# Adding the squares of the new x on VectorE before TensorE takes their column sums

## The chip, the cores and the metric

The kernel runs on one NeuronCore of a Trainium2 chip. The metric is device time in microseconds, from the start to the end of one execution. The profile names the engines PE (TensorE's matmuls), PEld (TensorE's weight loads), DVE (VectorE), ACT (ScalarE), POOL (GpSimd) and SP (SyncE, which issues the DMAs).

## The reference

A two-layer decoder trunk on 512 tokens of 1024 features, in float32. Layer 0 mixes tokens with dilated attention and an S5 state-space layer side by side, layer 1 with a gated linear recurrence (RG-LRU). Each mixer is followed by a SwiGLU feed-forward with 2816 hidden features.

```python
def rms_norm(x, g):
    return x * rsqrt(mean(x * x, axis=-1, keepdims=True) + 1e-6) * g

for layer in range(2):
    hn = rms_norm(x, norm_mix_pre[layer])
    mix = even_mixer(hn, ...) if layer % 2 == 0 else odd_mixer(hn, ...)   # both end in  y @ w_out
    x = x + rms_norm(mix, norm_mix_post[layer])
    hn = rms_norm(x, norm_ffn_pre[layer])
    ff = (silu(hn @ w_gate[layer]) * (hn @ w_up[layer])) @ w_down[layer]
    x = x + rms_norm(ff, norm_ffn_post[layer])
```

So there are four places where a product is normed, added to x, and the new x is normed again for the next stage. Three of them go through the function that is changed here; the fourth, behind the last feed-forward, writes the output and has no next norm.

## The kernel before

x is kept transposed: eight tiles `xT[f]` of 128 features (partitions) by 512 tokens. A float32 product is made of three matmuls of split operands, high times high, low times high, high times low; so each weight and each activation has a `hi` part, which ScalarE writes, and a `lo` part, which VectorE writes as the difference.

`out_proj` (L414) makes the output projection of a stage, the norm after it, the addition to x and the operands of the next stage. It is called three times: for layer 0's mixer (its tiles read `mo`, the products that follow `mo0b`), for layer 0's feed-forward (`fd`, then `fd0b`) and for layer 1's mixer (`mo` again, then `mo1b`). Below, these are mo0, fd and mo1. The product of the last four weight rows is done for the two halves of the tokens one after the other, 256 columns each, and `norm_half(h)` (L472) then works on half h while TensorE goes on with the other half, and after that with the next stage's products of the half that is done (`half_cols`, L549).

For a half, `cs` (L170 through `col_sums`) sums the squares of the product o over the features; `rst` on VectorE (L378 or L380) and `rsy` on POOL (L381) make the reciprocal root of it; `bc` broadcasts it over the partitions by TensorE. Then, for each of eight feature tiles f:

- L490, VectorE: o = o * gain * bc
- L496, POOL (for f = 0 VectorE, L494): xT += o
- L497, ScalarE: `xh`, the high part of the next operand
- L500, ScalarE: the square of the new x, into `nsq`
- L485, VectorE: `xl`, the low part, some tiles later

The squares must be summed over all 1024 features for the norm ahead of the next stage. TensorE does it: `next_sums` (L468) takes, for each tile and each 128 tokens, the square as the weights and a column of ones as the moving operand, and adds up in the bank `ns`. That is 16 matmuls for a half, 32 for a call, 96 in all; each leaves two records in the trace. They are issued for two tiles together, one pair of tiles late, so that the squares are mostly ready. When a call's `ns` is complete, `rst_f` (or `rst_m`), `rsy_f` and `bc_f` follow from it as above.

TensorE, VectorE and ScalarE each take their instructions strictly in their own queue's order. While `in_order` is set, which is from the tail of the projection through the first `half_cols` of the next stage, the instructions of `out_proj` on these engines keep the order in which the program states them (`pe.pin`, `seq_of`). When the steps of `norm_half` come in between the matmuls is set by due times on a clock that counts the matmuls stated with `pe.matmul` (`NORM_CS`, `NORM_BC`, `NORM_F`); `next_sums` states its own with `pe.pin` and moves no clock. All other instructions, those of the feed-forward and of layer 1, are placed by a scheduler, and shift when its picture of the engines shifts.

The two feed-forwards follow mo0 and mo1. They make most of their products by the Winograd form of Strassen's scheme (seven products of half blocks), so VectorE forms sums of weights (L638 to L641) and of activations (L660 to L663), ScalarE casts them to high parts (`whi`, L240; `th`, L667) and VectorE makes the low parts (`wlo`, L241; `tl`, L668). Behind fd stand plain products for layer 1, of 512 columns each.

## Time and profile before

| | |
|---|---|
| time, median of 3 runs | 1176.76 us (1175.7 to 1180.08) |
| profiled execution | 1172.18 us |
| its span | 1170.2 us |
| mean granted TensorE clock | 0.995 |
| busy: PE, PEld, DVE, ACT, POOL | 1129.9, 1010.3, 878.1, 629.2, 60.5 us |
| first and last group of `ns` matmuls starts in mo0, fd, mo1 | 266.5 and 290.5, 626.4 and 651.8, 797.2 and 824.3 us |

The span runs from the first to the last instruction on the profile's clock; the execution's own time is 2.0 us longer. "Busy" of an engine is the time in which at least one of its instructions runs. An idle time in square brackets at a row's end names the instruction that ended it. Times of single rows are from the span's start.

### The profile page before, as it was taken

The numbers are of one execution on the slowest core, as the hardware profiler recorded it, in microseconds if no ns is written. First come the engines' busy times: TensorE is split into PE (matmuls) and PEld (weight loads), VectorE is DVE, ScalarE is ACT, GpSimd is POOL, SyncE is SP. The second block draws the span as 40 slices with busy tenths as digits, with TensorE's granted clock in tenths as the row PEclk, the third lists the DMA queues.
The fourth block names the chain that finished last, engine by engine and source line by source line (L and its number), as shares of the span: only waits on it lengthen the run. The fifth ranks groups of instructions, "written<-read, shape, count | busy, mean of one in ns | idle before, by whom it ended". The sixth has DMA issues, their size and how long they took to land.

```text
span 1170.2 us, 20253 instructions
## 1 busy us (share of the span) xinstructions
PE 1129.9 (97%) x7550; PEld 1010.3 (86%) x7550; DVE 878.1 (75%) x1841; ACT 629.2 (54%) x1290; POOL 60.5 (5%) x101
## 2 busy tenths in 40 slices
PE   6899999999999999999999999999999999999997
PEld 6777766789899999988889987889999999988886
DVE  7978875567999899983445896966999899994224
ACT  7556567446754545662243469744955455582221
POOL 2000010004000000000002200004000000000001
PEclk9899999999999999999999999999999999999999
DMA  8254420431343323332340333340253343234221
GB/s 214 97 147 123 104 73 1 141 95 28 110 119 97 91 85 106 94 121 92 114 121 1 91 91 90 121 132 1 73 144 95 91 118 95 85 123 123 93 63 72
DMA packets 165273, 113.45 MB, mean 97 GB/s; under 512 B 26820, under 2 KB 141752, under 8 KB 165176
## 3 DMA queue, kind: packets, MB, share of 16 engines
q1 hardware_dynamic: 161848, 109.94, 32.2%
q10 hardware_dynamic: 3040, 2.17, 0.7%
q8 instruction: 59, 0.97, 0.4%
q14 instruction: 38, 0.31, 0.1%
q0 software_dynamic: 288, 0.07, 0.0%
HBM read 103.75 MB, written 4.19 MB: 92 GB/s over the span
## 4 chain that ended last, share of the span: by engine, by line
PE 78%; ACT 8%; DMA 6%; DVE 5%; issue 2%; POOL 1%; SPq 0%; ACTq 0%; DVEq 0%; POOLq 0%
PE fo L170 10%; PE op_fd L170 10%; PE qkv L170 5%; PE f00b L170 5%; PE f02b L170 5%; PE f01b L170 4%; PE f11b L170 4%; PE op_mo L170 4%; PE f12b L170 4%; PE f10b L170 4%; PE gg L170 3%; PE f03b L170 2%; PE f13b L170 2%; PE xbb L170 2%; PE fd0b L170 2%
## 5 line engine op out<-in xcount | busy, mean ns | idle before, releaser
L241 DVE TENSOR_TENSOR wlo_fo<-wraw_fo,whi_fo 128x512 fp32r<-128x512 f32 x44 | 30.2, 691 | 63.6 <-PE fo L170 55.4
L170 PE MATMUL op_fd<-hi_f,whi_fd 128*128 128x512 f32 (+1 forms) x200 | 73.6, 368 | 0.0
L170 PE MATMUL op_fd<-lo_f,whi_fd 128*128 128x512 f32 (+1 forms) x200 | 73.3, 366 | 0.0
L170 PE MATMUL op_fd<-hi_f,wlo_fd 128*128 128x512 f32 (+1 forms) x200 | 72.9, 368 | 0.0
L170 PE MATMUL fo<-wlo_fo,hi_f 128*128 128x512 f32 x176 | 69.6, 395 | 0.0
L170 PE MATMUL fo<-whi_fo,lo_f 128*128 128x512 f32 x176 | 69.2, 394 | 0.0
L170 PE MATMUL fo<-whi_fo,hi_f 128*128 128x512 f32 x176 | 68.9, 396 | 0.0
L240 ACT ACTIVATE whi_fo<-wraw_fo 128x512 fp32r<-128x512 f32 x44 | 27.6, 631 | 70.2 <-DMA wraw_fo<-in_ffn_w_down_dram 43.8
L241 DVE TENSOR_TENSOR wlo_fd<-wraw_fd,whi_fd 128x512 fp32r<-128x512 f32 x44 | 30.0, 690 | 46.5 <-ACT whi_fd L240 40.4
L240 ACT ACTIVATE whi_fd<-wraw_fd 128x512 fp32r<-128x512 f32 x44 | 27.4, 629 | 55.0 <-DMA wraw_fd<-in_ffn_w_down_dram 34.2
L170 PEld LDWEIGHTS op_fd<-lo_f,whi_fd 128*128 128x128 f32 x200 | 37.7, 189 | 6.9
L170 PE MATMUL qkv<-whi_qkv,xh_m 128*128 128x512 f32 x96 | 42.1, 440 | 1.5 <-DVE up L1200 1.3
L170 PEld LDWEIGHTS op_fd<-hi_f,wlo_fd 128*128 128x128 f32 x200 | 37.7, 188 | 6.7
L170 PEld LDWEIGHTS op_fd<-hi_f,whi_fd 128*128 128x128 f32 x200 | 37.7, 188 | 6.5
L170 PE MATMUL qkv<-wlo_qkv,xh_m 128*128 128x512 f32 x96 | 39.2, 408 | 2.6 <-DVE wlo_qkv L241 2.6
L170 PEld LDWEIGHTS fo<-whi_fo,lo_f 128*128 128x128 f32 x176 | 33.1, 188 | 7.8
L170 PEld LDWEIGHTS fo<-whi_fo,hi_f 128*128 128x128 f32 x176 | 33.1, 188 | 7.7
L170 PEld LDWEIGHTS fo<-wlo_fo,hi_f 128*128 128x128 f32 x176 | 33.1, 188 | 7.5
L170 PE MATMUL qkv<-whi_qkv,xl_m 128*128 128x512 f32 x96 | 39.0, 407 | 0.0
L638 DVE TENSOR_TENSOR wraw_s_f<-wraw_f,wraw_f 128x512 f32<-128x512 f32 x40 | 27.3, 683 | 10.6 <-DMA wraw_f<-in_ffn_w_up_dram 7.5
L241 DVE TENSOR_TENSOR wlo_mo<-wraw_mo,whi_mo 128x512 fp32r<-128x512 f32 x32 | 21.4, 685 | 15.3 <-ACT whi_mo L240 15.1
L639 DVE TENSOR_TENSOR wraw_t_f<-wraw_s_f,wraw_f 128x512 f32<-128x512 f32 x40 | 27.2, 681 | 5.6 <-DMA wraw_f<-in_ffn_w_gate_dram 5.6
(1975 smaller groups left out, 4289.2 us busy)
## 6 DMA issues: line engine op xcount, KB each, us to landing
wraw_f<-in_ffn_w_gate_dram SPq DMA_DIRECT2D x88, 256.0 KB, 3.2
wraw_f<-in_ffn_w_up_dram SPq DMA_DIRECT2D x88, 256.0 KB, 3.4
wraw_fd<-in_ffn_w_down_dram SPq DMA_DIRECT2D x44, 256.0 KB, 2.7
wraw_fo<-in_ffn_w_down_dram SPq DMA_DIRECT2D x44, 256.0 KB, 2.9
wraw_qkv<-in_ev_w_in_dram SPq DMA_DIRECT2D x24, 256.0 KB, 3.5
wraw_mo<-in_ev_w_out_dram SPq DMA_DIRECT2D x16, 256.0 KB, 5.2
wraw_xb<-in_od_w_in_dram SPq DMA_DIRECT2D x16, 256.0 KB, 2.9
wraw_gg<-in_od_w_in_dram SPq DMA_DIRECT2D x16, 256.0 KB, 2.9
```

Of the source, the lines that this page charges most:

```text
L170: self.pin(nc.tensor.matmul(o, lhsT=lhsT, rhs=rhs, start=start, stop=stop, **kw))
L240: act.activation(hi, src, AF.Copy)
L241: eng.tensor_tensor(lo, src, hi.bitcast(F32), op=ALU.subtract)
L638: dve.tensor_tensor(s1, a21, a22, op=ALU.add)
L639: dve.tensor_tensor(s2, s1, a11, op=ALU.subtract)
```

## The change

The squares get four buffers for each half, of 128 by 256. Tile 0's square goes into the fourth, `sq[3]`, which then serves as the running total; the others rotate through the first three. VectorE adds each square to the total, one tile late (the add of tile f−1 is stated after the square of tile f), seven adds for a half. When the total is complete, TensorE takes its column sums with two matmuls, one for each 128 tokens, which start and stop by themselves. So a half has 2 `ns` matmuls and not 16, and 7 adds; over three calls 84 matmuls go and 42 adds come. Squares, xh, xl, o and POOL's adds are the same in number. Behind L500 line numbers become six smaller.

```diff
-        def next_sums(h, fs, q):
-            for i, f in enumerate(fs):
-                for t in range(2):
-                    c = 2 * h + t
-                    pe.pin(nc.tensor.matmul(nsum[:, c:c + 1], lhsT=q[:, i * HT + t * P:i * HT + (t + 1) * P],
-                                            rhs=ones[:, 0:1], start=(c == 0 and f == 0), stop=(f == NF - 1),
-                                            skip_group_check=True))
...
+            sq = [sb.tile([P, S], F32, tag="sqacc" if h else "sq", bufs=2, name=f"nsq_{nm}{h}{i}") for i in range(2)]
+            sq = [q[:, HS[i]] for q in sq for i in range(2)]
...
-                if f % 2 == 0:
-                    q = sb.tile([P, S], F32, tag="sqacc" if h else "sq", bufs=2, name=f"nsq_{nm}{h}{f}")
-                seq_of(act.activation(q[:, HS[f % 2]], xf, AF.Square))
+                seq_of(act.activation(sq[f % 3] if f else sq[3], xf, AF.Square))
+                if f > 1:
+                    seq_of(dve.tensor_tensor(sq[3], sq[3], sq[(f - 1) % 3], op=ALU.add))
                 late.append(f)
-                if f % 2 and f > 1:
-                    next_sums(h, (f - 3, f - 2), qlast)
-                if f % 2:
-                    qlast = q
                 ready.update((h, q) for q in range(late[0]))
                 yield NORM_F
-            next_sums(h, (NF - 2, NF - 1), qlast)
+            seq_of(dve.tensor_tensor(sq[3], sq[3], sq[(NF - 1) % 3], op=ALU.add))
+            for t in range(2):
+                c = 2 * h + t
+                pe.pin(nc.tensor.matmul(nsum[:, c:c + 1], lhsT=sq[3][:, t * P:(t + 1) * P], rhs=ones[:, 0:1],
+                                        start=True, stop=True))
```

VectorE's queue in fd, from o of tile 4 of the first half (`o_fd_7376` before, `o_fd_7358` after) to the o of tile 7; `rst` belongs to the second half. Before:

```order
L490 SCALAR_TENSOR_TENSOR o_fd_7376<-o_fd_7376,cols,bc_fd_7588 128x256
L485 SCALAR_TENSOR_TENSOR xl_fd_7442<-xT_179,cols,xh_fd_7434 128x256
L490 SCALAR_TENSOR_TENSOR o_fd_7378<-o_fd_7378,cols,bc_fd_7588 128x256
L485 SCALAR_TENSOR_TENSOR xl_fd_7443<-xT_180,cols,xh_fd_7435 128x256
L490 SCALAR_TENSOR_TENSOR o_fd_7380<-o_fd_7380,cols,bc_fd_7588 128x256
L485 SCALAR_TENSOR_TENSOR xl_fd_7444<-xT_181,cols,xh_fd_7436 128x256
L380 SCALAR_TENSOR_TENSOR rst_fd_7729<-cs_fd_7724,eps_f_3386 128x2
L490 SCALAR_TENSOR_TENSOR o_fd_7382<-o_fd_7382,cols,bc_fd_7588 128x256
```

and after:

```order
L484 SCALAR_TENSOR_TENSOR o_fd_7358<-o_fd_7358,cols,bc_fd_7570 128x256
L479 SCALAR_TENSOR_TENSOR xl_fd_7424<-xT_179,cols,xh_fd_7416 128x256
L494 TENSOR_TENSOR nsq_fd_7574<-nsq_fd_7574,nsq_fd_7573 128x256
L484 SCALAR_TENSOR_TENSOR o_fd_7360<-o_fd_7360,cols,bc_fd_7570 128x256
L479 SCALAR_TENSOR_TENSOR xl_fd_7425<-xT_180,cols,xh_fd_7417 128x256
L494 TENSOR_TENSOR nsq_fd_7574<-nsq_fd_7574,nsq_fd_7573 128x256
L484 SCALAR_TENSOR_TENSOR o_fd_7362<-o_fd_7362,cols,bc_fd_7570 128x256
L479 SCALAR_TENSOR_TENSOR xl_fd_7426<-xT_181,cols,xh_fd_7418 128x256
L494 TENSOR_TENSOR nsq_fd_7574<-nsq_fd_7574 128x256
L380 SCALAR_TENSOR_TENSOR rst_fd_7706<-cs_fd_7701,eps_f_3368 128x2
L484 SCALAR_TENSOR_TENSOR o_fd_7364<-o_fd_7364,cols,bc_fd_7570 128x256
```

Between every two o now stands an add of a square, the square of the tile ahead of the last o; `rst` stands behind the add of tile 5's square. The order of mo1 is the same.

TensorE's queue in fd at the sums of the first half (`fd0b` are products of layer 1 from tiles that are done), before:

```order
L170 MATMUL fd0b_7669<-xh_fd_7435,whi_xb_0_7412 128x256
L170 MATMUL fd0b_7669<-xh_fd_7435,wlo_xb_0_7413 128x256
L468 MATMUL ns_fd_7448<-ones,nsq_fd_7718 128x1 x4
L170 MATMUL fd0b_7670<-xh_fd_7435,whi_xb_0_7424 128x256
L170 MATMUL fd0b_7670<-xh_fd_7435,wlo_xb_0_7425 128x256
```

and after:

```order
L170 MATMUL fd0b_7649<-xh_fd_7417,whi_xb_0_7394 128x256
L170 MATMUL fd0b_7649<-xh_fd_7417,wlo_xb_0_7395 128x256
L501 MATMUL ns_fd_7430<-ones,nsq_fd_7574 128x1 x2
L170 MATMUL fd0b_7650<-xh_fd_7417,whi_xb_0_7406 128x256
L170 MATMUL fd0b_7650<-xh_fd_7417,wlo_xb_0_7407 128x256
```

The last sums of the half keep their place among the products of tile 3, ahead of the `bc` of the second half; three groups of four ahead of them are gone.

VectorE's queue at the end of mo0's second half, where the feed-forward's work begins (`wraw`, `wlo` are weights). Before:

```order
L490 SCALAR_TENSOR_TENSOR o_mo_2936<-o_mo_2936,cols,bc_mo_3272 128x256
L485 SCALAR_TENSOR_TENSOR xl_mo_2999<-xT_182,cols,xh_mo_2991 128x256
L485 SCALAR_TENSOR_TENSOR xl_mo_3000<-xT_183,cols,xh_mo_2992 128x256
L639 TENSOR_TENSOR wraw_t_f_0_3505<-wraw_s_f_0_3503,wraw_f_0_3495 128x512
L241 TENSOR_TENSOR wlo_f02a_3511<-wraw_f_0_3495,whi_f02a_3510 128x512
L641 TENSOR_TENSOR wraw_s_f_4_3504<-wraw_f_4_3497,wraw_t_f_0_3505 128x512
```

and after:

```order
L484 SCALAR_TENSOR_TENSOR o_mo_2936<-o_mo_2936,cols,bc_mo_3264 128x256
L479 SCALAR_TENSOR_TENSOR xl_mo_2999<-xT_182,cols,xh_mo_2991 128x256
L494 TENSOR_TENSOR nsq_mo_3268<-nsq_mo_3268,nsq_mo_3267 128x256
L633 TENSOR_TENSOR wraw_t_f_0_3487<-wraw_s_f_0_3485,wraw_f_0_3477 128x512
L635 TENSOR_TENSOR wraw_s_f_4_3486<-wraw_f_4_3479,wraw_t_f_0_3487 128x512
L498 TENSOR_TENSOR nsq_mo_3268<-nsq_mo_3268,nsq_mo_3267 128x256
L479 SCALAR_TENSOR_TENSOR xl_mo_3000<-xT_183,cols,xh_mo_2992 128x256
L479 SCALAR_TENSOR_TENSOR xl_mo_3001<-xT_184,cols,xh_mo_2993 128x256
L241 TENSOR_TENSOR wlo_f02a_3493<-wraw_f_0_3477,whi_f02a_3492 128x512
```

The first low parts of weights (`wlo_f02a`) now stand behind the last add and all xl; on ScalarE the five casts that begin the feed-forward (`whi_f02a`, `whi_f02c`, `whi_f02d`) likewise stand behind the last square, where four of them stood ahead of it.

## The prediction

> **What bounds the kernel now.** I read the page's busy times first, then the chain that ended last, the table by stretches, the list of TensorE's waits, and last the rows around the three norms.
>
> ```profile
> span 1170.2 us, 20253 instructions
> PE 1129.9 (97%) x7550; PEld 1010.3 (86%) x7550; DVE 878.1 (75%) x1841; ACT 629.2 (54%) x1290; POOL 60.5 (5%) x101
> PE 78%; ACT 8%; DMA 6%; DVE 5%; issue 2%; POOL 1%; SPq 0%; ACTq 0%; DVEq 0%; POOLq 0%
> ```
>
> TensorE is busy 97% of the span and holds 78% of the chain, so work taken off it should count at first sight. The table by stretches (its columns: stretch, length, busy time of PE, PEld, DVE, ACT and POOL with counts, clock, DMA share, GB/s) shows where that fails:
>
> ```profile
> 272.00:283.00 11.00, 11.00 (x96) 11.00 (x96) 7.46 (x18) 6.43 (x16) 6.28 (x9) 1.00 0.01 1
> 283.00:296.00 13.00, 13.00 (x113) 13.00 (x112) 12.71 (x31) 12.34 (x25) 2.83 (x4) 1.00 0.43 122
> 296.00:340.00 44.00, 41.73 (x344) 40.92 (x344) 43.69 (x87) 28.99 (x60) 0.00 (x0) 1.00 0.36 103
> 652.00:664.00 12.00, 12.00 (x89) 11.30 (x88) 8.17 (x27) 5.24 (x9) 1.01 (x1) 1.00 0.46 132
> 664.00:700.00 36.00, 36.00 (x157) 29.12 (x156) 33.40 (x59) 22.50 (x36) 0.00 (x0) 1.00 0.34 103
> 824.00:836.00 12.00, 10.78 (x89) 10.53 (x90) 10.70 (x29) 12.00 (x26) 1.07 (x1) 1.00 0.54 153
> 836.00:900.00 64.00, 62.58 (x517) 61.45 (x517) 63.73 (x126) 37.60 (x76) 0.00 (x0) 1.00 0.36 100
> ```
>
> Behind mo0 (283 to 340) VectorE has 0.6 us free in 57, and TensorE is the one that idles. Behind mo1 ScalarE is full to 836, then VectorE. Behind fd (652 to 700) TensorE is full, and VectorE has 6.4 us to spare. The granted clock is 1.00 throughout and moves no term. TensorE's waits from 266 to 330 (engine and line, whom it waited for, total, times, longest), from 625 to 740, and the first and third from 795 to 900:
>
> ```profile
> PE f01b L170 <- ACT pu_f L703: 1.2, 1, 1.2
> PE f02b L170 <- ACT whi_f03c L240: 0.9, 1, 0.9
> PE mo0b L170 <- DVE xl_mo L485: 0.7, 1, 0.7
> PE ns_mo L468 <- ACT nsq_mo L500: 0.4, 1, 0.4
> ```
> ```profile
> PE ns_fd L468 <- ACT nsq_fd L500: 0.8, 3, 0.3
> ```
> ```profile
> PE f11b L170 <- DVE tl_f L668: 1.2, 1, 1.2
> PE ns_mo L468 <- ACT nsq_mo L500: 0.8, 3, 0.3
> ```
>
> Both feed-forward starts (f01b, f02b, f11b) already wait for VectorE or ScalarE. From 625 to 740 only the column sums of fd wait.
>
> **Removed from TensorE.** Of 32 column-sum matmuls a call, 4 stay. A group of four (eight records) among its neighbours:
>
> ```profile
> 280.64 0.29 PE L170 MATMUL mo0b<-xh_mo,wlo_f 128*128 128x256 f32 x1
> 280.77 0.95 PE L468 MATMUL ns_mo<-ones,nsq_mo 128*128 128x1 f32 x8
> 281.57 0.37 PE L170 MATMUL mo0b<-xh_mo,whi_f 128*128 128x256 f32 x1
> 281.78 0.28 PE L170 MATMUL mo0b<-xh_mo,wlo_f 128*128 128x256 f32 x1
> ```
>
> From the matmul before it to the second one after it are 1.14 us, of which two ordinary steps of 0.12 are 0.24. So the group costs 0.90 and one matmul 0.225. A half loses 14 of them, 3.15 us; a call 6.3; all 84 are 18.9. The waits at ns in the list, 0.4 and twice 0.8, come on top: 20.9 if all of it reached the end.
>
> **Added to VectorE.** There are 42 adds of 128x256, a shape that the feed-forward has too:
>
> ```profile
> 289.93 0.41 DVE L661 TENSOR_TENSOR wraw_tr_f<-xb_f,xa_f 128x256 f32<-128x256 f32 x1
> 290.26 0.41 DVE L662 TENSOR_TENSOR wraw_tr_f<-xb_f,wraw_tr_f 128x256 f32<-128x256 f32 x1
> ```
>
> One takes 0.41, and the next starts 0.34 after it: 14.3 us in all, 4.8 a call. Where they stand matters more. The add of tile f−1 precedes o of tile f+1 in VectorE's fixed order, and it waits for its square. So every o hangs on the o two tiles ahead through a whole loop: o, POOL's add, xh, square, add. The rows of that loop:
>
> ```profile
> 646.05 0.47 DVE L490 SCALAR_TENSOR_TENSOR o_fd<-o_fd,cols,bc_fd 128x256 f32<-128x256 f32 x1
> ...
> 646.93 0.47 DVE L490 SCALAR_TENSOR_TENSOR o_fd<-o_fd,cols,bc_fd 128x256 f32<-128x256 f32 x1
> ```
> ```profile
> 643.36 5.12 POOL L496 TENSOR_TENSOR xT<-xT,o_fd 128x256 f32<-128x256 f32 x6 [0.75 <-DVE o_fd L490]
> ```
> ```profile
> 632.86 0.51 ACT L497 ACTIVATE xh_fd<-xT,cols 128x256 fp32r<-128x256 f32 x1
> 633.27 0.40 ACT L500 ACTIVATE nsq_fd<-xT 128x256 f32<-128x256 f32 x1
> ```
>
> Now a tile takes 0.88 (646.05 to 646.93). The loop is o 0.47, POOL 0.85 (5.12 for six), xh 0.41 until the square starts, square 0.40, add 0.34, and three handoffs, for which I estimate 0.05 each: 2.62 for two tiles, 1.31 for one. Seven steps lengthen a half by 3.0 us.
>
> **fd, first half.** VectorE and TensorE:
>
> ```profile
> 627.39 0.43 DVE L526 TENSOR_TENSOR oacc_fd<-oacc_fd,oqs_fd 128x256 f32<-128x256 f32 x1 [1.45 <-ACT oqs_fd L524]
> 627.73 0.87 DVE L490 SCALAR_TENSOR_TENSOR o_fd<-o_fd,cols,bc_fd 128x256 f32<-128x256 f32 x2
> ...
> 634.06 0.16 DVE L380 SCALAR_TENSOR_TENSOR rst_fd<-cs_fd,eps_f 128x2 f32<-128x2 f32 x1 [1.82 <-PE cs_fd L170]
> 634.14 0.47 DVE L490 SCALAR_TENSOR_TENSOR o_fd<-o_fd,cols,bc_fd 128x256 f32<-128x256 f32 x1
> ```
> ```profile
> 636.90 0.60 PE L468 MATMUL ns_fd<-ones,nsq_fd 128*128 128x1 f32 x4 [0.34 <-ACT nsq_fd L500]
> ```
>
> The o of tile 2 stays at 627.73, as it stands behind an oacc add that waited for ScalarE. Its square is done 2.2 later (0.47, 0.85, 0.41, 0.40 and handoffs), at 629.95; the add of it and one o+=op put tile 4 at about 630.65, and one loop more puts tile 6 at 633.3. Tile 3 follows tile 2 at 628.47 (0.40 + 0.34), tile 5 at about 631.9, and so the add of square 5 ends near 634.5. In the new order the rst of the second half stands behind that add: 634.55 instead of 634.06. Today rst waits 1.82 for column sums; TensorE will have these some 1.7 earlier, so that wait is merely replaced by the add's. From o of tile 7 to ns it takes 2.76 now (634.14 to 636.90), and 3.2 with an add and its handoff. ns starts at 637.85, 0.9 later than now. TensorE is there near 633.4 and waits about 4 us in place of 0.8. **The saving of the first half is gone, and 0.9 with it.** In the second half bc comes 0.9 later. ns is ready 11.5 us after the first o (seven steps of 1.31, and 2.3 for the last tile's POOL add, xh, square and add), while TensorE has 113 matmuls of 0.12, 13.6 us, to do before: no wait, and the 3.15 are saved. fd gives −2.2. VectorE ends this half 3 us late, but it idles 3.8 in 652 to 664, which covers that; without this cover TensorE would stand up to 0.8. The bounds are −4.4, if rst follows the column sums at once, and 0, if a loop is 0.3 a tile longer than I make it.
>
> **mo0.** No oacc add holds up tile 2 here. Twelve of the removed matmuls and the 0.4 wait stand ahead of bc. I estimate that o of the second half starts 1.8 earlier; ns, behind that o on VectorE, then takes most of this back. So TensorE ends the first half 0.4 ahead and the second 3.5. VectorE's first feed-forward work comes 1.2 us late (3.0 longer, 1.8 earlier start), and so do ScalarE's five weight casts, now behind the last square. In return the program's new order lifts ut ahead of other ScalarE work. The ends are −3.5 (TensorE's lead is kept) and +1.2 (the lag is passed on whole). I take −0.5, a little to the right of the middle, since VectorE's 43.69 of 44 leaves it little to catch up with.
>
> **mo1.** The first half goes as in fd. TensorE arrives 2.2 early and VectorE 3.0 late. One idle time there is to be won back:
>
> ```profile
> 833.45 0.69 DVE L638 TENSOR_TENSOR wraw_s_f<-wraw_f,wraw_f 128x512 f32<-128x512 f32 x1 [1.30 <-PE f10b L170]
> ```
>
> The ends are −2.2 and +3.0. I take +0.3, near the middle, as no row is nearer to one of them.
>
> **Sum.** −0.5 − 2.2 + 0.3 = −2.4. The profiled execution took 1172.18 (the span of 1170.2 and 2.0 around it), so it would be 1169.8. It lies 4.6 below the median shown; on that median of 1176.76 the forecast is **1174.4**.
>
> **A rule against the change.** While POOL adds, VectorE's xl, with two inputs, stretches:
>
> ```profile
> L485 DVE SCALAR_TENSOR_TENSOR xl_fd<-xT,cols,xh_fd x16: 472/558/917, 625.1 to 649.4; 128x256 fp32r<-128x256 f32 x16
> ```
> ```profile
> 641.98 0.92 DVE L485 SCALAR_TENSOR_TENSOR xl_fd<-xT,cols,xh_fd 128x256 fp32r<-128x256 f32 x1 [0.19 <-ACT xh_fd L497]
> ```
> ```profile
> 641.87 0.74 POOL L496 TENSOR_TENSOR xT<-xT,o_fd 128x256 f32<-128x256 f32 x1 [5.87 <-DVE o_fd L490]
> ```
>
> At least it takes 0.47, in the median 0.56, and 0.92 where it starts just behind a POOL add. By the median an added add costs 0.09 more, 3.8 us over all 42; by the longest row 0.45 more. The Trainium skill, "SBUF — State Buffer", section "Who interferes with whom", says that a VectorE instruction with two SBUF inputs contends with a GpSimd one that reads SBUF, and that the first to issue blocks the other fully. The 0.92 agrees with a full block; the median does not reach it.
>
> **Rivals.** A, *TensorE's lead is kept everywhere*: at the feed-forward starts the new order serves TensorE first, and weights that are not needed yet slip instead. For it: waits of only some 2 us at the first start, 97% busy. Against it: VectorE's 43.69 and 63.73. It gives −3.5 − 2.2 − 2.2 = −7.9, 1168.9, and with fd at −4.4, 1166.7. B, *slower*: VectorE's lag reaches TensorE at both feed-forward starts, and the adds meet POOL's. Without contention that is +1.2 − 2.2 + 3.0 = +2.0; with the longest row, seven adds of 0.45 more in the second half of mo0 and of mo1, 3.2 each, it is +8.4, 1185.2. It decides once the two lags together pass 2.2 us. For it: the full VectorE. Against it: 0.56 is the usual row. C, *nothing comes of it*: fd's gain is lost too, because TensorE stands 6 us at fd's ns and not 4, and the two starts cancel: 0, 1176.8. That TensorE loses its 84 matmuls is not in doubt.
>
> **Chances.** Forecast 0.42, A 0.25, B 0.20, C 0.13. A measurement of this kernel can tell about 0.5%, 5.9 us, from no change. Faster by more: all but a little of A and a tenth of the forecast, 0.27. Slower by more: over half of B, 0.12. Within: 0.61. The range reaches A with the better fd and two thirds into B, 1166.5 to 1182; the forecast's own is 1171 to 1178.
>
> **What would show it.** Right: ns waits for VectorE about 1.5 us in mo0 and 4 in fd and in mo1; the o of fd's second half stand 1.3 apart; TensorE stays full from fd's end on; VectorE is full behind mo0. Wrong: ns in fd waits under 2 us (nearer A), the adds read 0.6 or more (B), or TensorE's idle time behind mo0 or mo1 differs by more than 3 us from now.

## The result, and the profile after

| | before | after |
|---|---|---|
| median | 1177.49 us (4 runs, 1175.7 to 1180.08) | 1192.58 us (4 runs, 1189.62 to 1197.55) |
| profiled execution | 1172.18 us | 1192.71 us |
| its mean granted clock | 0.995 | 0.980 |

The ratio is 1.0133, with a 95% interval of 1.0101 to 1.0164: the kernel became about 15 us slower. The forecast was 1174.4 us with a range of 1166.5 to 1182, so the result lies above the range, on the side to which 0.12 was given.

The head of the page of the changed kernel, which answers to the three lines quoted first in the prediction:

```profile
span 1190.9 us, 19959 instructions
PE 1128.3 (95%) x7382; PEld 1004.2 (84%) x7382; DVE 902.2 (76%) x1883; ACT 632.2 (53%) x1290; POOL 63.2 (5%) x101
PE 74%; DVE 10%; DMA 6%; ACT 5%; issue 3%; POOL 1%; SPq 0%; ACTq 0%; DVEq 0%; POOLq 0%
```

168 matmul records fewer, and yet TensorE is busy for only 1.6 us less: some of its matmuls became longer. VectorE has 24.1 us more, where 42 adds of 0.34 make 14.3. Its share of the chain went from 5% to 10%. The same stretches as before, with one more in fd (640 to 652) and one in layer 1 (700 to 740):

```profile
272.00:283.00 11.00, 8.66 (x58) 8.30 (x58) 9.29 (x23) 5.61 (x14) 5.46 (x8) 0.84 0.01 1
296.00:340.00 44.00, 38.08 (x294) 36.56 (x293) 40.92 (x85) 30.02 (x63) 1.00 (x1) 0.96 0.36 103
640.00:652.00 12.00, 7.99 (x47) 7.99 (x48) 5.08 (x13) 2.44 (x6) 2.76 (x4) 0.72 0.00 0
664.00:700.00 36.00, 36.00 (x168) 29.64 (x168) 34.13 (x85) 19.86 (x31) 1.01 (x1) 1.00 0.30 89
700.00:740.00 40.00, 36.88 (x147) 29.26 (x146) 28.93 (x44) 34.41 (x54) 0.00 (x0) 0.91 0.31 92
836.00:900.00 64.00, 55.91 (x441) 53.06 (x440) 63.80 (x131) 45.24 (x91) 4.30 (x4) 1.00 0.35 99
```

TensorE loses 3.6 us more than before behind mo0 (38.08 in place of 41.73) and 6.7 more behind mo1 (55.91 in place of 62.58). mo1 starts 10.6 us later here than before; with the stretch moved by that, from 846.6 to 910.6, it is 57.17, a loss of 5.4. In the middle of fd it is busy for 8 of 12 us, at a granted clock of 0.72. TensorE's waits:

```profile
PE ns_mo L501 <- DVE nsq_mo L498: 7.5, 3, 5.4
PE ns_fd L501 <- DVE nsq_fd L498: 5.4, 1, 5.4
PE f01b L170 <- ACT pu_f L697: 3.8, 4, 3.0
PE rg L170 <- ACT gr L1542: 3.1, 1, 3.1
```

The columns are the sum of the waits, their number and the longest. In each of fd and mo1 it stands 5.4 us at once for the total of the first half; rg, a product of layer 1, has a wait that was not there before. The reason for the long stand is in the rows of VectorE and POOL. In the second half of fd:

```profile
653.82 0.47 DVE L484 SCALAR_TENSOR_TENSOR o_fd<-o_fd,cols,bc_fd 128x256 f32<-128x256 f32 x1
654.22 0.47 DVE L479 SCALAR_TENSOR_TENSOR xl_fd<-xT,cols,xh_fd 128x256 fp32r<-128x256 f32 x1
654.61 0.95 DVE L494 TENSOR_TENSOR nsq_fd<-nsq_fd 128x256 f32<-128x256 f32 x1
655.49 0.47 DVE L484 SCALAR_TENSOR_TENSOR o_fd<-o_fd,cols,bc_fd 128x256 f32<-128x256 f32 x1
655.88 0.47 DVE L479 SCALAR_TENSOR_TENSOR xl_fd<-xT,cols,xh_fd 128x256 fp32r<-128x256 f32 x1
656.27 0.95 DVE L494 TENSOR_TENSOR nsq_fd<-nsq_fd,nsq_fd 128x256 f32<-128x256 f32 x1
657.15 0.47 DVE L484 SCALAR_TENSOR_TENSOR o_fd<-o_fd,cols,bc_fd 128x256 f32<-128x256 f32 x1
```
```profile
654.37 0.91 POOL L490 TENSOR_TENSOR xT<-xT,o_fd 128x256 f32<-128x256 f32 x1 [0.75 <-DVE o_fd L484]
656.04 0.91 POOL L490 TENSOR_TENSOR xT<-xT,o_fd 128x256 f32<-128x256 f32 x1 [0.75 <-DVE o_fd L484]
```

Both adds start 0.23 or 0.24 us after one of POOL's adds, and take 0.95 and not 0.41. Of all 42 adds 26 start 0.09 to 0.25 us behind an add of POOL. They take 0.89 to 0.96 us, and each ends 0.28 or 0.29 after that add of POOL has ended. The other 16 take 0.41 to 0.43. The meeting comes back tile after tile, because the order itself brings the two together: the end of an o sets POOL off, and behind that o on VectorE stand one xl and then the add. A tile takes 1.67 us (653.82, 655.49, 657.15). VectorE idles nowhere in it: from start to start o takes 0.40, xl 0.39 and the add 0.88. What follows from it at the end of fd's first half, on VectorE before and after, and on TensorE after:

```profile
640.46 0.48 DVE L490 SCALAR_TENSOR_TENSOR o_fd<-o_fd,cols,bc_fd 128x256 f32<-128x256 f32 x1 [3.40 <-PE bc_fd L170]
```
```profile
643.53 0.42 DVE L498 TENSOR_TENSOR nsq_fd<-nsq_fd,nsq_fd 128x256 f32<-128x256 f32 x1 [1.46 <-ACT nsq_fd L492]
649.98 0.48 DVE L484 SCALAR_TENSOR_TENSOR o_fd<-o_fd,cols,bc_fd 128x256 f32<-128x256 f32 x1 [5.23 <-PE bc_fd L170]
```
```profile
644.01 1.01 PE L501 MATMUL ns_fd<-ones,nsq_fd 128*128 128x1 f32 x4 [5.39 <-DVE nsq_fd L498]
...
646.31 0.41 PE L170 MATMUL fd0b<-xh_fd,whi_xb 128*128 128x256 f32 x1
646.52 0.41 PE L170 MATMUL fd0b<-xh_fd,wlo_xb 128*128 128x256 f32 x1
...
649.30 0.65 PE L170 MATMUL bc_fd<-cst,rsy_fd 128*128 128x128 f32 x4
...
651.21 0.28 PE L170 MATMUL fd0b<-xh_fd,whi_xb 128*128 128x256 f32 x1
651.32 0.28 PE L170 MATMUL fd0b<-xh_fd,wlo_xb 128*128 128x256 f32 x1
```

The bc of the second half stands behind ns in TensorE's queue. So VectorE, which is to start the second half, waits for TensorE, which waits for VectorE's total. And after the stand TensorE's matmuls follow one another every 0.21 us and not every 0.12, until past 649, so that bc comes 5.3 us behind ns where it was 2.9 (636.90 to 639.81). VectorE idles 5.23 us there in place of 3.40.

### The profile page after: what moved, and what is told of

It is laid out like the page before. It is cut to its first block, busy times and chain, and to the rows that moved or that the text cites. A ratio compares the mean times of both kernels' runs of the same rounds, so it can differ in the third digit from the quotient of the medians.

```text
span 1190.9 us, 19959 instructions
## 1 busy us (share of the span) xinstructions
PE 1128.3 (95%) x7382; PEld 1004.2 (84%) x7382; DVE 902.2 (76%) x1883; ACT 632.2 (53%) x1290; POOL 63.2 (5%) x101
## 4 chain that ended last, share of the span: by engine, by line
PE 74%; DVE 10%; DMA 6%; ACT 5%; issue 3%; POOL 1%; SPq 0%; ACTq 0%; DVEq 0%; POOLq 0%
PE fo L170 10%; PE op_fd L170 10%; PE f01b L170 4%; PE f11b L170 4%; PE f00b L170 4%; PE f12b L170 4%; PE qkv L170 4%; PE f02b L170 4%; PE f10b L170 4%; PE op_mo L170 3%; PE gg L170 3%; PE f13b L170 2%; PE f03b L170 2%; PE xbb L170 2%; PE fd0b L170 2%
## 5 line engine op out<-in xcount | busy, mean ns | idle before, releaser
L491 ACT ACTIVATE xh_mo<-xT,cols 128x256 fp32r<-128x256 f32 x32 | 16.3, 509 | 36.5 <-POOL xT L490 24.8
L241 DVE TENSOR_TENSOR wlo_mo<-wraw_mo,whi_mo 128x512 fp32r<-128x512 f32 x32 | 21.5, 688 | 16.9 <-ACT whi_mo L240 16.7
```

The source lines that it names most:

```text
L241: eng.tensor_tensor(lo, src, hi.bitcast(F32), op=ALU.subtract)
L491: seq_of(act.activation(xh[f][:, HS[h]], xf, AF.Copy, scale=col(gname, glayer * NF + f)))
```

## The experiments

All kernels but e3 in one table. Between the two columns of lag and the three of stretches the reader can see which follows which. The stretches are taken from the starts of groups of matmuls in each trace: mo0 with its feed-forward (first `mo0b` to first `cs_fd`), fd with layer 1 (to the first `mo1b`), mo1 with its feed-forward (to the first `fo`). The lag is the start of VectorE's first low part of a feed-forward weight (`wlo_f02a`, `wlo_f12a`), counted from the first `mo0b` or `mo1b`. All but the first row are differences to before, in us.

| kernel | time to before, ratio | lag, mo0 | mo0 and ffn | fd and layer 1 | lag, mo1 | mo1 and ffn |
|---|---|---|---|---|---|---|
| before | | 21.5 | 354.8 | 180.0 | 21.2 | 238.6 |
| after | 1.0133 [1.0101, 1.0164] | +5.6 | +5.1 | +5.4 | +11.5 | +9.9 |
| e6, fd alone | 1.0058 [1.0035, 1.008] | +1.5 | +1.6 | +7.6 | +1.6 | +1.1 |
| e7, mo0 alone | 1.0039 [1.0015, 1.0064] | +5.6 | +3.5 | +2.8 | +2.9 | +2.6 |
| e8, mo1 alone | 1.0078 [1.0046, 1.0109] | +1.5 | +1.4 | +0.4 | +10.8 | +10.0 |
| e1, sums stated late | 1.0053 [1.0031, 1.0075] | +5.6 | +3.6 | −1.0 | +6.7 | +4.7 |
| e2, total in PSUM | 1.0103 [1.008, 1.0126] | +4.0 | +3.7 | +1.9 | +8.5 | +9.7 |
| e4, late sums, late adds | 1.0027 [1.0003, 1.0051] | +4.6 | +5.3 | −3.4 | +5.7 | +5.6 |
| e5, no adds | 0.9927 [0.99, 0.9953] | −1.6 | −0.8 | −4.3 | +3.6 | +1.2 |
| e12, adds alone | 1.0116 [1.0081, 1.0151] | +12.6 | +10.7 | +4.1 | +9.4 | +7.0 |
| e10, stand filled | 1.0136 [1.0098, 1.0173] | +5.6 | +6.2 | +4.4 | +9.2 | +8.7 |
| e9, best form at fd | 0.998 [0.9958, 1.0002] | +0.1 | +0.6 | −1.9 | +2.9 | +2.4 |
| e11, first halves | 0.9994 [0.997, 1.0017] | −0.9 | +1.5 | −3.9 | +0.2 | −0.9 |

Three limits of the table. A stretch that a kernel does not change still differs by up to 2.8 us between profiles, so little below 3 us can be read from one row. The clock goes with it: these stretches are 0.4 to 1.6 longer where it read 0.50 once for 3.4 us (e6 at mo0 and mo1, e8 at mo0 and fd), and 2.4 to 2.8 longer where it did for 6.8 us (e7 at fd and mo1, e9 at mo1). The profiled execution of the kernel before lies 5.3 us under the median, and from mo0 to fo its clock does not fall once. So the differences come out large: those of the changed kernel add up to 20.4 us, where the medians are 15 apart. And the part ahead of mo0, which no version changes, takes from 262.5 to 271.5 us; so the table compares stretches, and the ratios, which are of all runs and not of the profiled ones, need not agree with their sums.

**e1: is it the stand at the first half's ns?** The first half's two sums are stated together with those of the second half, so TensorE does not stand there and bc is not behind them.

```diff
-            for t in range(2):
-                c = 2 * h + t
-                pe.pin(nc.tensor.matmul(nsum[:, c:c + 1], lhsT=sq[3][:, t * P:(t + 1) * P], ...
+            total[h] = sq[3]
+            for c in range(NT if h else 0):
+                pe.pin(nc.tensor.matmul(nsum[:, c:c + 1], lhsT=total[c // 2][:, c % 2 * P:(c % 2 + 1) * P], ...
...
```

> The changed kernel, but the two column-sum matmuls of the first half are stated together with those of the second half; in TensorE's queue they move some 55 matmuls back, behind the bc of the second half. Adds and their places on VectorE stay. Theory W (the loss is TensorE standing 5.4 us at the first half's sums in fd and in mo1, and 2.3 in mo0, in its fixed order, and running at a granted clock of 0.5 for some 6 us after each stand): no wait at ns above 1 us, bc of fd's second half some 7 us earlier, clock 1.00 in all three places; 1171 to 1179 us, so about as the kernel before. Theory L (the loss is VectorE's: adds that take 0.95 and not 0.42 beside POOL make each half 5 us longer, and the next stage starts late): TensorE stands as long at xl or at the feed-forward's weights instead; 1186 us or more.

Measured: 1179.74 us beside 1174.69 of before, 1.0053. TensorE's waits:

```profile
PE ns_mo L502 <- DVE nsq_mo L499: 1.8, 2, 1.3
PE ns_fd L502 <- DVE nsq_fd L499: 1.0, 1, 1.0
```

The long stands are gone (1.3 us is left in mo1), and with them 0.8 of the 1.33%, some 9 us. The time lies just above theory W's range and well below theory L's. The kernel is still slower than before: having the sums ahead of bc is the larger part of the loss and not the whole.

**e2: is the add long because of POOL?** The running total is kept in PSUM, so that an add reads only one operand from SBUF.

```diff
+            tot = nsum[:, HT:S]
...
-                seq_of(act.activation(sq[f % 3] if f else sq[3], xf, AF.Square))
+                seq_of(act.activation(sq[f % 3] if f else tot, xf, AF.Square))
                 if f > 1:
-                    seq_of(dve.tensor_tensor(sq[3], sq[3], sq[(f - 1) % 3], op=ALU.add))
+                    seq_of(dve.tensor_tensor(tot, tot, sq[(f - 1) % 3], op=ALU.add))
...
-            seq_of(dve.tensor_tensor(sq[3], sq[3], sq[(NF - 1) % 3], op=ALU.add))
+            seq_of(dve.tensor_tensor(sq[3], tot, sq[(NF - 1) % 3], op=ALU.add))
```

> The changed kernel, but the running total of the squares lies in PSUM (in the unused half of the bank that takes the column sums) and only the last add writes SBUF. Each add then has one SBUF input and not two. Number and order of all instructions are as in the changed kernel. If the adds' 0.95 comes from a second SBUF input while POOL adds: adds of 0.42 to 0.50 throughout, o of fd's second half 1.3 apart and not 1.67, ns waits of about 3 us and not 5.4 in fd and mo1; theory L expects 1180 to 1185 us, theory W 1183 to 1188 (shorter stands, the clock still falls at times). If the 0.95 has another cause: adds stay at 0.95, time within 3 us of the changed kernel.

Measured: 1186.39 us, 1.0103. The norm of the next stage comes out differently in this kernel, so only its durations are used. VectorE's rows in the second half of fd:

```profile
649.79 0.47 DVE L485 SCALAR_TENSOR_TENSOR o_fd<-o_fd,cols,bc_fd 128x256 f32<-128x256 f32 x1
650.94 0.43 DVE L495 TENSOR_TENSOR ns_fd<-ns_fd,nsq_fd 128x256 f32<-128x256 f32 x1 [0.28 <-ACT nsq_fd L493]
651.28 0.47 DVE L485 SCALAR_TENSOR_TENSOR o_fd<-o_fd,cols,bc_fd 128x256 f32<-128x256 f32 x1
652.14 0.43 DVE L495 TENSOR_TENSOR ns_fd<-ns_fd,nsq_fd 128x256 f32<-128x256 f32 x1
652.48 0.47 DVE L485 SCALAR_TENSOR_TENSOR o_fd<-o_fd,cols,bc_fd 128x256 f32<-128x256 f32 x1
```

The same add takes 0.43 us, and 0.42 where it starts 0.23 us behind an add of POOL (in mo0, at 267.45); a tile takes 1.35 (two tiles from 649.79 to 652.48). So 0.95 is the price of the second SBUF operand beside POOL's add, and without that the predicted loop of 1.31 is right: VectorE idles 0.28 before every second add, for its square. TensorE's wait at fd falls only to 4.1, the 4 that was predicted; and the time falls by some 3 us, with intervals that overlap. It is within theory W's range and above theory L's. The length of the add decides the size of the stand, and the place of the sums that there is one. So an add and a loop of the predicted size leave the kernel 1.03% slower than before: the larger error of the prediction lies behind them.

**e3: can the adds be taken out of the loop by stating each a tile later?**

```diff
-                if f > 1:
-                    seq_of(dve.tensor_tensor(sq[3], sq[3], sq[(f - 1) % 3], op=ALU.add))
+                if f > 2:
+                    seq_of(dve.tensor_tensor(sq[3], sq[3], sq[(f - 2) % 3], op=ALU.add))
...
-            seq_of(dve.tensor_tensor(sq[3], sq[3], sq[(NF - 1) % 3], op=ALU.add))
+            for f in (NF - 2, NF - 1):
+                seq_of(dve.tensor_tensor(sq[3], sq[3], sq[f % 3], op=ALU.add))
```

> The changed kernel, but each square is added two tiles late and not one: the add of tile f-2 stands ahead of o of tile f+1, and two adds stand at the end of a half. The loop of o, POOL, xh, square and add then spans three tiles. Tiles about 1.05 us apart (3.1 over 3) where they were 1.67. Theory W: the stands at ns shrink from 5.4 to some 2 us, short enough for the clock to hold at least in part; 1177 to 1184 us. Theory L: VectorE's halves are 4 us shorter, 1175 to 1182. Neither theory: no change of more than 3 us.

Measured: 1194.63 us, the median of three runs, 1.0165 [1.0125, 1.0206], so not better than the changed kernel, which is the third alternative. The profiled execution took 4017 us, with matmuls of 128x512 near 1 us that take 0.39 in the other profiles, so TensorE's waits can't be read from it. VectorE's rows in the second half of fd can:

```profile
2250.47 0.47 DVE L484 SCALAR_TENSOR_TENSOR o_fd<-o_fd,cols,bc_fd 128x256 f32<-128x256 f32 x1
2251.25 0.95 DVE L494 TENSOR_TENSOR nsq_fd<-nsq_fd 128x256 f32<-128x256 f32 x1
2252.13 0.47 DVE L484 SCALAR_TENSOR_TENSOR o_fd<-o_fd,cols,bc_fd 128x256 f32<-128x256 f32 x1
```

A tile still takes 1.66, and not the expected 1.05, and the adds still meet POOL's. With an add of 0.95 it is not the loop through POOL and ScalarE that spaces the tiles, but VectorE's own three instructions. e4, which states its adds in the same way, has the same 1.66. By e3's order the last two adds of a half also stand together ahead of the same ns.

**e4: e1 and e3 together.**

> Both edits together: sums of the first half stated with those of the second, adds two tiles late. If the waits in TensorE's order and the length of VectorE's halves are all that stands between the removed 18.9 us of matmuls and the end: 1162 to 1170 us, faster than the kernel before. If the feed-forward starts stay bound by VectorE whatever TensorE gains: 1172 to 1178 us.

Measured: 1178.81 us, 1.0027. TensorE's waits:

```profile
PE f01b L170 <- ACT pu_f L699: 4.7, 4, 2.9
PE f11b L170 <- ACT pu_f L699: 3.7, 5, 1.6
PE ns_mo L503 <- DVE nsq_mo L500: 0.7, 1, 0.7
PE ns_fd L503 <- DVE nsq_fd L500: 0.5, 1, 0.5
```

The waits at ns are down to 0.7 and 0.5, and fd with layer 1 gains 3.4. But the feed-forward starts wait more (f01b had 2.1 before, f11b 0.5 for pu), and both stretches are over 5 us longer than before. The first alternative of the expectation, a gain, is ruled out, and the time lies 0.8 above the second; the loss sits where VectorE comes late to the feed-forward.

**e5: what is TensorE's saving worth without any add?** All adds are left out, and only the last square is summed.

```diff
-                if f > 1:
-                    seq_of(dve.tensor_tensor(sq[3], sq[3], sq[(f - 1) % 3], op=ALU.add))
...
-            seq_of(dve.tensor_tensor(sq[3], sq[3], sq[(NF - 1) % 3], op=ALU.add))
...
-                pe.pin(nc.tensor.matmul(nsum[:, c:c + 1], lhsT=sq[3][:, t * P:(t + 1) * P], ...
+                pe.pin(nc.tensor.matmul(nsum[:, c:c + 1], lhsT=sq[(NF - 1) % 3][:, t * P:(t + 1) * P], ...
```

> The changed kernel without its 42 adds: TensorE takes the column sums of the last tile's square alone, two matmuls a half at the same place. The other seven squares of a half are left out of the sum. TensorE's 84 matmuls are gone, VectorE has the work of the kernel before. Theory V (the feed-forward starts lose because the adds make VectorE late): the two feed-forward stretches come back to within 2 us of the kernel before (322.6 us from the end of mo0b to the sums of fd, 208.0 from the end of mo1b to fo), and the time is 1158 to 1166 us. Theory S (they lose because the scheduler places their instructions in another order, whatever VectorE has to do): both stay 5 us or more longer, 1168 to 1176.

Measured: 1166.45 us beside 1175.92, 0.9927. TensorE's waits:

```profile
PE ns_mo L498 <- ACT nsq_mo L492: 2.3, 2, 2.1
PE ns_fd L498 <- ACT nsq_fd L492: 2.1, 1, 2.1
PE rg L170 <- ACT gr L1539: 0.2, 1, 0.2
```

Of the 18.9 us of matmuls that TensorE no longer does, about 8.6 reach the end. In the profile fd with layer 1 gains 4.3, and the other two stretches nothing that can be told from zero, with 6.3 us less of TensorE's work each. But the profiled execution took 9.2 us more than the median, and its clock read 0.50 for 6.8 us in each of these two stretches, where that of the kernel before did not fall; so a gain of one or two us there is not excluded. The sign that theory V named came at mo1 alone: from the end of mo1b to fo takes 209.6 us, 1.6 longer than before, but from the end of mo0b to the sums of fd 327.5, 4.9 longer. mo0b itself ended 5.7 earlier, so at mo0 what TensorE won was given back behind it. That fits a start bound by VectorE and ScalarE, as the prediction read it from the table by stretches. The time lies 0.45 above theory V's range and below theory S's. Between e5 and the changed kernel are 2.06%, 24 us, all of which the adds brought, directly or through waits.

**e6, e7, e8: each place alone.** The new form at fd, at mo0 or at mo1, the old form at the other two.

> The change at fd alone; mo0 and mo1 sum as before. If the losses of the three places add up as the two traces show them (fd +1.3, layer 1's mixer behind it +4.1, with a new wait of 3.1 us for the gate gr): 5 us slower than before, 1178 to 1182. If the wait in layer 1 comes from the way in which the whole program is placed, and not from fd: 0 to 2 slower.

> The change at mo0 alone. If the losses add up (mo0 itself -1.2, the feed-forward behind it +6.4): 5 us slower than before, 1178 to 1182. Theory S would give a stretch from mo0b's end to fd's sums that is as long as in the changed kernel, theory V as well; what tells here is whether layer 1 and mo1, which do not have the change, keep their old lengths (140.3 and 30.6 us).

> The change at mo1 alone. If the losses add up (mo1 itself +3.2, the feed-forward behind it +6.7): 10 us slower than before, 1182 to 1187, and with e6 and e7 about 20 in all, more than the 15 that the runs of the changed kernel show in the median. If the three overlap: less.

Measured: 1.0058, 1.0039 and 1.0078, which is 1181.80, 1180.41 and 1183.98 us, each within the range given for losses that add up. Each place loses by itself, fd too, where the prediction had its one clear gain. The three sum to 1.75%, more than the 1.33% of all together, though the intervals allow that they are equal. In e7 the unchanged fd and mo1 are 2.8 and 2.6 longer, at a granted clock that fell to 0.60 and 0.57 there for some 8 us, so part of each single loss may be of that kind.

**e9: the best form at fd alone.** The form of e4 at fd, the old one at mo0 and mo1.

> New form at fd alone, its adds two tiles late and the first half's two sums stated with the second half's; mo0 and mo1 as before. If fd's saving is real and only the waiting at ns, its clock and the late add spoiled it: fd and layer 1 together take 176 to 178 us in place of 180.0, waits at ns_fd under 1, and the time is 1171 to 1173 (2 to 4 below the kernel before, here taken as 1175). If VectorE's later end at fd reaches layer 1 in any case (the wait of rg for gr stays at 2 or more), fd and layer 1 take 179 to 181 and the time is within 1 us of the kernel before.

Measured: 1174.31 us beside 1175.16, 0.998 with an interval to 1.0002. That is the second expectation, within 1 us of before, though the interval takes in the first. fd with layer 1 takes 178.1, at the edge of the first; rg still waits 2.8, as the second has it. fd itself takes 35.6 in place of 40.3, and layer 1 142.5 in place of 139.7, so 2.8 of the 4.7 us are given back behind fd.

**e10: does the fallen clock have a price of its own?** The changed kernel, with throwaway matmuls ahead of the first half's ns, so that TensorE is not idle there.

```diff
+            if h == 0:
+                for i in range({"mo0": 12, "fd0": 40, "mo1": 40}[nm]):
+                    pe.pin(nc.tensor.matmul(nsum[:, HT:S], lhsT=first[0](0)[0], rhs=xh[0][:, HS[0]], ...
```

> The changed kernel, with 40 throwaway matmuls of 128x256 ahead of the first half's ns in fd and in mo1 and 12 in mo0, so that TensorE stands there for little (under 1 us) but gains nothing in work. If the clock that falls after the stand has a cost of its own: the granted clock from 640 to 652 reads 0.95 or more instead of 0.72, the fd stretch falls from 41.5 to about 39, and the time by 3 to 7 us, to 1186 to 1190. If VectorE's lag sets the ends whatever TensorE does: the stretches of fd and mo1 shorten, but the wait of rg and the feed-forward stretches take it back, and the time stays within 2 us of the changed kernel (1190 to 1194).

Measured: 1191.43 us, 1.0136. The stretch in the middle of fd, and TensorE's waits:

```profile
640.00:652.00 12.00, 11.30 (x95) 11.10 (x95) 7.48 (x18) 3.94 (x10) 3.52 (x6) 1.00 0.00 1
```
```profile
PE rg L170 <- ACT gr L1545: 4.1, 2, 3.1
PE ns_fd L504 <- DVE nsq_fd L498: 0.7, 1, 0.7
```

The clock is 1.00 again, the fd stretch is 39.5 and not 41.5, and the time is within 2 us of that of the changed kernel, which is the second expectation. At fd 1.0 of the 2.0 us goes at once into a longer wait of rg. I had come to hold the clock for a cause beside the stand, worth 2.5 us at each place; that theory falls, for this kernel. What remains of it lies within the interval, which is 4 us to either side.

**e11: only the first halves.** Adds two tiles late, the total summed ahead of the second half's old sums; the second halves as before.

```diff
+            new = h == 0
...
+                    if f == 3:
+                        for c in range(2):
+                            pe.pin(nc.tensor.matmul(nsum[:, c:c + 1], lhsT=total[0][:, c * P:(c + 1) * P], ...
```

> New form in the first halves only (adds two tiles late, the two sums stated ahead of the second half's old ones); the second halves as before. If what delays the feed-forward starts is the second half's adds and late end on VectorE: nothing is late there, mo0 with its feed-forward stays near 355 and mo1 with its own near 239, fd gains 3, and the time is 1171 to 1173 against 1175. If the first half's longer loop delays the reciprocal root and broadcast of the second half (by 1 to 1.5 us each) and with it VectorE's end: each feed-forward start loses 1 to 1.5, fd gains 2, and the time is 1175 to 1177.

Measured: 1174.45 us beside 1175.16, 0.9994 [0.997, 1.0017]: neither gain nor loss. The lags are −0.9 and +0.2, mo1 with its feed-forward does not lengthen, and fd with layer 1 is 3.9 shorter, which the first expectation has; its 2 to 4 us of gain in the median don't show. The time lies between the two ranges. e4, whose adds in the first half are the same, has lags of 4.6 and 5.7. So without adds in the second half VectorE comes to the feed-forward in time, and the loss is gone.

**e12: the adds alone.** The kernel before, with all its sums on TensorE, and the 42 adds into a total that nobody reads.

```diff
+            tot = sb.tile([P, HT], F32, tag=f"sqtot{h}", bufs=1, name=f"ntot_{nm}{h}")
...
+                if f == 2:
+                    seq_of(dve.tensor_tensor(tot, prev[0], prev[1], op=ALU.add))
+                elif f > 2:
+                    seq_of(dve.tensor_tensor(tot, tot, prev[f - 1], op=ALU.add))
...
+            seq_of(dve.tensor_tensor(tot, tot, prev[NF - 1], op=ALU.add))
```

> The kernel before, all of its sums on TensorE, plus the 42 adds at the places that the change gives them, into a total that nobody reads. If the adds themselves delay VectorE's feed-forward work and that is most of the loss: mo0 with its feed-forward 4 to 6 us longer than 354.8, mo1 with its own 4 to 8 longer than 238.6, fd and layer 1 up to 3 longer, 1184 to 1191 in all. If the loss comes from TensorE standing at ns for the total: nobody waits for these adds, ns waits stay near 1, and the time is 1175 to 1179.

Measured: 1188.35 us, 1.0116. Three rows of VectorE in fd, and the stretch after mo0's first half:

```profile
658.12 0.95 DVE L507 TENSOR_TENSOR ntot_fd<-ntot_fd,nsq_fd 128x256 f32<-128x256 f32 x1
659.00 0.47 DVE L492 SCALAR_TENSOR_TENSOR o_fd<-o_fd,cols,bc_fd 128x256 f32<-128x256 f32 x1
659.79 0.95 DVE L507 TENSOR_TENSOR ntot_fd<-ntot_fd,nsq_fd 128x256 f32<-128x256 f32 x1
```
```profile
272.00:283.00 11.00, 11.00 (x61) 11.00 (x61) 4.43 (x11) 3.26 (x8) 1.97 (x3) 0.60 0.01 1
```

The time is that of the first expectation: nobody waits for the total, and the loss is nearly that of the whole change. The old sums do wait more, 2.1 in fd and 1.9 in mo0 and mo1 together; that the squares come as late as the o is the likely reason. A tile of o, xl and add takes 1.67 us here too. mo0 and fd are longer than that expectation has it (10.7 and 4.1). In this profile mo0's stretch bears half of the loss, with a clock of 0.60, and the clock falls in fd and mo1 too, so lags and stretches of this row are in part the clock's, and their split over the places is that of one execution.

**What the table says together.** Where VectorE comes late to its feed-forward work, the stretch is longer by about as much: by 0.6 to 1.2 times the lag in all rows where the lag is 4 us or more, and by nothing that can be told from zero where it is under 1. Lag and stretch also go together in e10, where the clock stayed up through the three norms, and in e12, where TensorE did all its old work. They do so too in the unchanged places where the clock fell (lags of 1.5 to 2.9), so the relation alone does not tell the cause; that adds are the cause is told by e5 and e11, where the loss goes with the adds that are left out. For fd the traces show another relation. In before, e5, e7, e8, e11 and e12 TensorE's last `fd0b` starts 5.2 to 9.8 us after VectorE's last xl, and rg waits 0.2 us or not at all. In after, e1, e2, e4, e6, e9 and e10 it starts 2.0 to 2.1 after it, and rg waits 1.9 to 4.1. So TensorE had a cushion at fd, of work that VectorE had already prepared, and the change used it up. That the late operands of layer 1 come from this is the likely reading; no run changed that alone.

In percent, e5 (−0.73) and e12 (+1.16) add up to +0.43, close to e1 (+0.53), and the changed kernel has +1.33. The 0.8 to 0.9 between, some 10 us, goes with the place of the first half's sums; that it is what TensorE and VectorE lose by waiting for each other there is the reading that e1 supports.

One rival of all this is the granted clock. The experiments list 68 runs of the kernel before. Their times go with the mean clock, from 1170.7 us at 0.996 to 1182.7 at 0.983; a straight line through them gives 0.8 us for 0.001. The four runs of the changed kernel have 0.9815 on the mean, those of before 0.991. By that line, which is an estimate from these runs, about 7 of the 17.6 us between the means go with the clock, and at the same clock the changed kernel would still be about 10 us slower. A lower clock can follow from waits as well as cause a loss. In e10 the runs have 0.986, for which the line would give nearly 4 us, and the median is 1.2 us lower. How much of the 7 us the clock causes stays open.

## Why the prediction was wrong, step by step

**The adds cost 0.41 each: wrong.** 26 of the 42 cost 0.89 to 0.96, those that start just behind an add of POOL. The row of 0.92 was in the prediction, and so was the Trainium skill's rule ("SBUF — State Buffer", "Who interferes with whom"), that a VectorE instruction with two SBUF inputs contends with a GpSimd one that reads SBUF and the first to issue blocks the other; the forecast took the adds at 0.41, and the median of 0.56 of all xl kept the longer add for rival B. The 0.95 agrees with it, and the 0.43 of e2 with its other side in the same section: outside the two-port modes, VectorE with at most one SBUF input does not contend. The error was to treat the meeting as a matter of chance. The median mixed xl that stand anywhere; in the predicted loop, which names POOL's add as its second step, the add comes back just behind it, tile after tile. This is not the whole error: with adds of 0.43, e2 is still 12 us slower than before.

**The loop of 1.31 a tile: right only with the short add.** It is 1.35 in e2. In place a tile takes 1.67, and there the loop does not set it: with an add longer by 0.54 the prediction's loop would give 1.58, and VectorE's own o, xl and add take 1.67 without a pause. The three handoffs of 0.05 were set without a row; one of them, from the end of an o to POOL's add, is 0.08 (654.29 to 654.37). The second half of fd takes 4.0 us longer from its first to its last o, not 3.0.

**ns in fd waits about 4 us, bc comes 0.9 later: too small.** 4.1 in e2, 5.4 in place. The saving of the first half is gone, as predicted, and rst stands behind the add (640.81). But bc comes 4.3 us later, counted from the first column sums of the stage (20.9 before, 25.2 after): ns starts 1.9 and not 0.9 later, and the way from ns to bc is 2.4 longer because of the granted clock, which the prediction called a term that moves nothing. The Trainium skill has a rule for it ("TensorE: Matmul & The Clock Gate", Part 1): after an idle window of about 3.4 us TensorE runs at half rate. The trace agrees, with steps of 0.21 us behind the stand of 5.39. By e10 this costs little of the whole time, and rg's longer wait takes half of what it wins in fd.

**VectorE's late end at fd is covered by its 3.8 us of idle time: wrong.** Its last xl starts 9.0 us later after the first column sums (30.5 before, 39.5 after), while TensorE's last `fd0b` is 1.2 later. rg waits 3.1, and layer 1 takes 143.9 in place of 139.7. Instead of −2.2, fd with layer 1 gives +5.4. The bound of −4.4 is near what e5 measures without adds (−4.3), but there 3.1 of it lie in fd and 1.1 in layer 1, so this does not test the price of a removed matmul.

**mo0: −0.5 between −3.5 and +1.2. mo1: +0.3 between −2.2 and +3.0.** Measured: +5.1 and +9.9, both outside. This is the step that failed most: these two terms miss by 5.6 and 9.6, two thirds of what the three terms miss in the profiles. The prediction's end "the lag is passed on whole" is close to what happened. The lag itself was mis-sized: 1.2 expected and 5.6 measured in mo0, 3.0 and 11.5 in mo1, and 4.0 and 8.5 in e2, where adds, tile and stand have the predicted size. At mo1 the first half's stand delays the second half's bc as in fd, which the prediction had not counted there beyond 0.9.

**The rivals.** B, at 1185.2, was the right mechanism with its place, and too small, because it let adds meet POOL in two second halves only and left fd its gain. A is refuted by the changed kernel itself, whose two starts became longer; that they kept no lead even without adds is seen in e5's one profile, while e5's runs gain 8.6 us, near the 7.9 of A. C's stand of 6 us at fd came near (5.4), but what it costs there is more than the gain.

**What would show it.** The adds reading 0.6 or more was named as the sign of B, and TensorE's idle time behind mo0 or mo1 more than 3 us off as the sign of error; both appeared (0.95; 3.6 and 6.7). Right were ns in mo0 waiting about 1.5 us (1.67) and TensorE full from 664 to 700, though not from 700 to 740 (36.88 of 40, with rg's wait). Not seen were the o of fd's second half 1.3 apart (1.67), and a full VectorE behind mo0 (40.92 of 44).

## What to carry to other kernels

When an instruction is put into a fixed order, price it by the row that stands at the same phase to its neighbours on the other engines, and not by the median of its shape: a fixed order brings the same two instructions together tile after tile. Then set the loop through the engines beside the sum of each engine's own instructions; the longer of the two spaces the tiles. A sum that leaves TensorE for VectorE is worth what its place on VectorE allows: here the end of 18.9 us of matmuls gained 8.6 us with no adds, and with them the kernel lost 15. If a result is needed late, state its consumer late: two matmuls that nobody needed yet stood 5.4 us ahead of a broadcast for which VectorE waited, and to state them elsewhere recovered about 9 us.

## What the runs showed of the hardware that was not expected

The granted clock can fall after less idle time than the long stand. At ns in mo0, after two stands of 0.67 and 1.67 us within 4 us, the clock was 0.50 from 278 to 280:

```profile
274.81 0.68 PE L170 MATMUL bc_mo<-cst,rsy_mo 128*128 128x128 f32 x4 [0.67 <-DVE o_mo L484]
277.16 0.90 PE L501 MATMUL ns_mo<-ones,nsq_mo 128*128 128x1 f32 x4 [1.67 <-DVE nsq_mo L498]
```
```profile
276.00:278.00 2.00, 0.84 (x5) 0.84 (x5) 1.97 (x6) 1.30 (x4) 0.00 (x0) 0.83 0.00 0
278.00:280.00 2.00, 2.00 (x11) 2.00 (x11) 1.07 (x3) 0.70 (x2) 1.59 (x2) 0.50 0.04 8
```

In e12 it fell in mo0 after waits of 0.63 and 0.36 us and stayed at 0.50 from 268 to 280, with TensorE busy throughout. The kernel before waits 0.65 and 0.35 at the same place and keeps a clock of 1.00, so the length of these waits does not decide it alone; what does stays open. Unchanged stages with stands of under 1 us were hit in some profiles (e7 at fd and mo1) and not in others, so a single profile of this kernel carries up to 3 us a place of it. The Trainium skill's table ("TensorE: Matmul & The Clock Gate", Part 1) puts the change at one idle window of about 3.4 us; these stands are shorter, 2.34 us in sum in mo0 and 0.99 in e12, so here the measurement differs from that table.
